# Odd layer of a two-layer decoder trunk: q and k of a head group projected as a pair with seven block products, attention placed between parts of the next values' projection

## Chip, cores and metric

One Trainium2 chip, the kernel on one of its cores. The metric is the device time of one execution in microseconds (us). The kernel before takes 2124.32 us, the median of three runs (2123.64 to 2124.78).

## Reference

The trunk has two layers over a residual stream h of 256 positions and width 2048, all float32. The even layer (sliding-window attention beside a matrix memory) is untouched by the change. The odd layer and the feed-forward block that follows each mixer, cut to what matters:

```python
def forgetting_attention_mixer(xn, w_in, b_f, w_out):
    proj = xn @ w_in                              # 2048 x (2048 + 2048 + 2048 + 16)
    q, k, v, f = split_cols(proj, FOX_SIZES)      # 16 heads of 128
    ...
    log_f = jax.nn.log_sigmoid(f + b_f)
    c = jnp.cumsum(log_f, axis=1)
    ...
        s = q @ k.T * scale + c[query] - c[key]   # causal
        p = jax.nn.softmax(s, axis=-1)
        return p @ v
    ...
    return out @ w_out

h = h + mixer(rms_norm(h, norm_mix[layer]))
h = h + (silu(xn @ w_gate) * (xn @ w_up)) @ w_down   # hidden width 5632
```

## The kernel before

**Numbers as pairs.** Each float32 operand of a large projection is split into a rounded part "hi" and a remainder "lo". The product is three matmuls: hi by hi, hi by lo, lo by hi (lines 179 to 181 in `gemm`, 358 to 360 in `three`). Activations lie transposed in 16 k tiles of 128 (xh and xl for the normed stream, mh and ml for the mixer's or block's result). A weight chunk is two k tiles by 512 columns. It is loaded by the SP queue (`load_raw`, line 107) into one of four buffers "raw", rounded by ScalarE (line 151), and its remainder is made by VectorE (line 152). There are six buffers each for hi and lo. The 256 positions are two blocks of 128 rows (t = 0 and 1), and each accumulates in its own PSUM bank. There are eight banks: four under the tag "acc" (pool pa), four under "pm" (pool pm).

**Pairs with seven products.** In the feed-forward block two matrices are projected together (`pair_group`, line 365). For a pair of k tiles, two row blocks and two matrices make a 2 x 2 by 2 x 2 block product. A plain pair does all eight block products, 24 matmuls. A mixed pair (lines 389 to 419) forms sums of the blocks of x beforehand (`sums_of`, line 214) and differences of the weight blocks on VectorE (lines 396, 397, 401, 402), and does seven, 21 matmuls. Four banks "prod" collect products that must be recombined (lines 420 to 426). The table `ORDER` (line 36) says which of the eight k pairs are mixed: 2, 3 and 6. A pair group so takes all eight banks, four for the plain sums and four for the products.

**The odd layer** (lines 830 to 909). First a narrow projection of 272 columns yields the last two heads' values and the gates f. From the gates come the cumulative sums, which go through DRAM to be broadcast as the bias `cb1` of all 16 heads (2 MB, line 874), and two selections on GpSimd set the causal mask (line 877). Then four head groups of four heads follow. For each: q is projected alone (16 k tiles, 96 matmuls), scaled on ScalarE (line 836) and transposed per head on TensorE (`transpose_many`, line 261); k likewise; v is projected; and `attention` (line 268) does the scores (lines 275, 282), bias and scale on VectorE (276, 283), maximum (289), exponentials on ScalarE (304), normalisation (317), transposes of the probabilities (325, 329), the product with v (333, 334) and the split into mh and ml (343).

**Order of the work.** Each engine runs its instructions in the order of its own queue. The order is not that of the program text: a scheduler places instructions on the engines by its own model, so that those of a group's attention stand among the matmuls of the next projections. `close_layer` (line 550) opens the pool fp0 or fp1 for the rest of a layer (output projection, feed-forward block), in which the block sums `sx` of the normed stream lie too. The odd layer's pool "od" takes the room of the closed fp0.

Of the kernel before, what the change touches and what calls it, by code (L numbers as in the profile page):

```python
# [17 lines left out]
P = 128  # L18
# [21 lines left out]
}  # L40
DOWN_END = ((0, 0), (0, 1), (1, 2), (0, 3), (1, 4), (0, 5), (0, 6), (0, 7))
MID = 6
MID_DOWN = 5
# [11 lines left out]
def trunk(  # L55
# [48 lines left out]

    def load_raw(w, k0, c0, n, pool=wr):
        raw = pool.tile([P, CK, NB], F32, tag="raw", name="raw", bufs=4 if pool is wr else RAWS)
# [107 lines left out]
    def sums_of(pool, sh, sl, copies, full=None):  # L214
        if full is None:
            full = pool.tile([P, 2, NT, P], F32, tag="tmp", name="full")
            copies(full.rearrange("p i t q -> p i (t q)"))
        s = pool.tile([P, 4, P], F32, tag="tmp", name="s4")
        nc.vector.tensor_tensor(out=s[:, 0, :], in0=full[:, 0, 1, :], in1=full[:, 1, 1, :], op=ALU.add)
# [40 lines left out]

    def transpose_many(dst, srcs):
        m = len(srcs)
        pt = pm.tile([P, 4, P], F32, tag="pm", name="ptm")
# [4 lines left out]
    def attention(sp, q_of, k_of, v_of, dv, scale, bias0, bias1, k_tile, sinks=None, negc=None):  # L268
        s = sp.tile([P, 4, 3 * P], F32, tag="s", name="s", bufs=2)
        for half in range(2):  # L270
            hs = slice(half, 4, 2)
            p0 = pm.tile([P, 2, P], F32, tag="pm", name="p0")
            for jj in range(2):
                j = 2 * jj + half
                nc.tensor.matmul(p0[:, jj, :], q_of(j, 0), k_of(j)[:, 0:P], start=True, stop=True)
            nc.vector.scalar_tensor_tensor(
                out=s[:, hs, 0:P], in0=p0, scalar=scale, in1=bias0[:, hs, :], op0=ALU.mult, op1=ALU.add
            )
            p1 = pm.tile([P, 2, S], F32, tag="pm", name="p1")
# [34 lines left out]
        for b in range(NT):  # L314
            for j in range(4):
                e = s[:, j, parts[b]]
                nc.vector.tensor_scalar(e, e, rec[:, b, j : j + 1], None, op0=ALU.mult)
        t0 = sp.tile([P, 4, S], F32, tag="t0", name="t0", bufs=1)
        t1 = sp.tile([P, 4, P], F32, tag="t1", name="t1", bufs=1)
# [12 lines left out]
        def pv(po, j):  # L332
            nc.tensor.matmul(po, v_of(j, 0), t0[:, j, :], start=True, stop=False)  # L333
            nc.tensor.matmul(po[:, P : 2 * P], v_of(j, 1), t1[:, j, :], start=False, stop=True)

        per = P // dv
        for q in range(0, 4 // per, 2):
# [6 lines left out]

    def out_proj(w, idx, key, extra):
        last = KT - 4
        for n0 in (0, 2):
            accs = [new_acc() for _ in range(2)]
            for i in range(2):
                gemm(accs[i], m_of, w, (n0 + i) * NB, NB, 0, last, KT)  # L350
            for i in range(2):
# [12 lines left out]

    def pair_group(fp, par, lhs, sums, mats, order, todo=()):
        plain = [[bank(par, "acc") for _ in range(NT)] for _ in range(2)]
# [4 lines left out]
        for pos, (kind, pair) in enumerate(order):  # L371
# [18 lines left out]
            if first:  # L390
                prods = [bank(1 - par, "prod") for _ in range(4)]
            ra, rb = (load_raw(w, k0, c0, NB, fp) for w, c0 in mats)
            hg, lg = split_chunk(ra, NB)
            run_due(todo, pos)
            t4 = fp.tile([P, 2, NB], F32, tag="t4", name="t4", bufs=1)
            nc.vector.tensor_tensor(out=t4[:, 0, :], in0=rb[:, 0, :], in1=ra[:, 0, :], op=ALU.subtract)
# [7 lines left out]
            for two in (t4, rb):  # L404
                hs = fp.tile([P, 2, NB], F32R, tag="ht", name="ht")
                ls = fp.tile([P, 2, NB], F32R, tag="lt", name="lt")
# [12 lines left out]
            three(plain[0][1], xb[:, t1], lb[:, t1], ht[3], lt[3], False, False)  # L419
        c = fp.tile([P, 4, NB], F32, tag="c", name="c", bufs=1)  # L420
        u2 = fp.tile([P, NB], F32, tag="tmp", name="u2")
        nc.scalar.copy(c[:, 0, :], prods[0])
# [6 lines left out]
    def ffn(layer, fp, sx, sd, key, idx_next=None, key_next=None, finish=None):  # L429
        r = rstd(key)  # L430

        def sums_x(pair):
# [3 lines left out]
        for g0, g1 in zip(PARTS, PARTS[1:]):  # L436
# [4 lines left out]
            for g in range(g0, g1):  # L441
                par = (g1 - 1 - g) % 2
                plain, c = pair_group(
                    fp, par, x_of, sums_x, [(w_gate[layer], g * NB), (w_up[layer], g * NB)], ORDER, todo
                )
# [73 lines left out]
            for n0 in (0, 2):  # L519
                if end and idx_next is None and n0 == 2:  # L520
# [5 lines left out]
                plain, c = pair_group(  # L526
                    fp,
                    1 - n0 // 2,
# [20 lines left out]

    def close_layer(layer, w_out, idx, key, **rest):  # L550
        with tc.tile_pool(name=f"fp{layer}", bufs=2) as fp:
            nx = len(mixed_of(ORDER))
            nd = max(len(mixed_of(o)) for o in DOWN.values())
            sx = [fp.tile([P, nx, 4, P], F32R, name=f"sx{i}", bufs=1) for i in range(2)]
            sd = [fp.tile([P, nd, 4, P], F32R, name=f"sd{i}", bufs=1) for i in range(2)]
            out_proj(w_out, idx, key, (*sx, fp))
            ffn(layer, fp, sx, sd, key, **rest)
# [19 lines left out]
    with tc.tile_pool(name="ev", bufs=1) as ev:  # L577
# [22 lines left out]
        with tc.tile_pool(name="sw", bufs=1) as sw:  # L600
# [17 lines left out]
            def swa(g, qn):  # L618
# [14 lines left out]
                def half_of(j):  # L633
                    return slice((j % 2) * HD, (j % 2 + 1) * HD)

                attention(
                    sw,
# [8 lines left out]
                    sinks=sink[:, 4 * g : 4 * g + 4],  # L646
                )

# [67 lines left out]
        with tc.tile_pool(name="mp", bufs=1) as mp:  # L716
# [99 lines left out]
            for g in range(2):  # L816
# [8 lines left out]
                mlstm(2 * g + 1)  # L825

    close_layer(0, w_out_even[0], 2, "f0", idx_next=1, key_next="m1")


    r1 = rstd("m1")  # L830
    wi1 = w_in_odd[0]
    with tc.tile_pool(name="od", bufs=1) as od:
# [24 lines left out]
        nc.vector.scalar_tensor_tensor(out=nl, in0=fg, scalar=0.0, in1=nl, op0=ALU.min, op1=ALU.subtract)  # L857
        nc.vector.tensor_scalar(nl, nl, -1.0, None, op0=ALU.mult)
        pc = pm.tile([P, NB], F32, tag="pm", name="pcf")
        nc.tensor.matmul(pc[:, 0:FOX_H], upper, nl[:, 0, :], start=True, stop=True)  # L860
# [11 lines left out]
        nc.gpsimd.dma_start(scratch, negct)  # L872
        cb1 = od.tile([P, FOX_H, S], F32, name="cb1")
        nc.gpsimd.dma_start(cb1, scratch.partition_broadcast(P))
        cb0 = od.tile([P, FOX_H, P], F32, name="cb0")
        for dst, src in ((cb0, cb1[:, :, 0:P]), (cb1[:, :, P:S], cb1[:, :, P:S])):
            nc.gpsimd.affine_select(
                out=dst, in_=src, pattern=[[0, FOX_H], [-1, P]], compare_op=ALU.is_ge, fill=NEG, base=0, channel_multiplier=1
            )

        for i in range(4):
            qt = od.tile([P, 4, S], F32, tag="qt", name="qtf")
            kt = od.tile([P, 4, S], F32, tag="kt", name="ktf")
            for off, dst in ((0, qt), (FOX_H * FD, kt)):
                n_ = nat1(project(wi1, off + i * NB, NB), NB, "qk")
                for g in range(0, 4, 2):
                    transpose_many(
                        dst[:, g : g + 2, :].rearrange("p g (t q) -> p (g t) q", q=P),
                        [n_[:, t, (g + u) * FD : (g + u + 1) * FD] for u in range(2) for t in range(NT)],
                    )  # L890
# [6 lines left out]

            attention(
                od,
# [4 lines left out]
                FD**-0.5,  # L904
                cb0[:, 4 * i : 4 * i + 4, :],
                cb1[:, 4 * i : 4 * i + 4, :],
                4 * i,
                negc=negc[:, :, 4 * i : 4 * i + 4],
            )

# [29 lines left out]

    close_layer(1, w_out_odd[0], 3, "f1", finish=finish)

# [48 lines left out]
```

## Time and profile before

| | us |
|---|---|
| median of the runs | 2124.32 |
| profiled execution, its own time | 2125.9 |
| its span, first to last instruction | 2124.2 |
| TensorE (PE) busy | 2105.4 |
| VectorE (DVE) busy | 1709.8 |
| ScalarE (ACT) busy | 1252.2 |

The granted clock of TensorE was 0.998 of full speed on the mean. The odd layer's weights are loaded from 1014.5 us (first issue) on, and its four head groups are worked on from about 1062 to 1346 us.

The page's first part has busy time by engine. The second cuts the span into 40 slices of 53.1 us and gives busy tenths in each. The fourth follows what ended last back to the start. Queries of the trace give groups of instructions by line ("busy, mean ns of one, idle before them"), the waits of an engine and the timeline of a stretch. PE is TensorE's matmul, PEld its weight load, SP the queue that issues loads. A matmul's row is longer than the step from one to the next, since matmuls are pipelined. L152 is line 152 of the kernel.

### The profile page before, as it was taken

The page shows a single profiled execution, that of the slowest core. Times are in us where ns is not written, and L with a number is a line of the kernel's source. Part 1 is how long each engine was busy: PE and PEld are TensorE (multiplying, and loading weights), DVE is VectorE, ACT ScalarE, POOL GpSimd, SP SyncE. Part 2 cuts the span into 40 slices and gives each one's busy share as a digit, 9 for nine tenths or more (in the row PEclk, how much of TensorE's full clock was granted, in tenths as well). Part 3 has the DMA queues.
Part 4 walks back from the last instruction along what each step waited for, and adds up shares of the span by engine and source line. Part 5 has one row for each costly group of instructions (what it writes and reads, how often), then busy time and mean ns, then how long its engine had stood idle before and what let it go on. Part 6 is the DMA issues. An engine that isn't in the chain of part 4 may idle for free.

```text
span 2124.2 us, 26790 instructions
## 1 busy us (share of the span) xinstructions
PE 2105.4 (99%) x9708; PEld 1747.6 (82%) x9708; DVE 1709.8 (80%) x2204; ACT 1252.2 (59%) x1592; POOL 39.6 (2%) x61
## 2 busy tenths in 40 slices
PE   8999999999999999999999999999999999999998
PEld 6888888888888888888888888888888888888886
DVE  6665577899999999999755555668899998999995
ACT  6564455665577656666645444556755667556763
POOL 2010000000000000000010000000000000000000
PEclk9999999999999999999999999999999999999999
DMA  9454555766577666665575564656656767656763
GB/s 310 143 173 142 174 193 190 219 194 205 192 224 222 213 196 216 221 205 189 171 237 163 166 178 148 229 176 193 212 193 218 228 198 205 224 196 208 226 205 134
DMA packets 257989, 420.95 MB, mean 198 GB/s; under 512 B 56464, under 2 KB 64704, under 8 KB 257728
## 3 DMA queue, kind: packets, MB, share of 16 engines
q1 hardware_dynamic: 256976, 415.49, 61.5%
q0 software_dynamic: 736, 3.71, 0.6%
q8 instruction: 76, 1.25, 0.2%
q14 instruction: 57, 0.47, 0.1%
q10 hardware_dynamic: 144, 0.03, 0.0%
HBM read 406.57 MB, written 2.11 MB: 192 GB/s over the span
## 4 chain that ended last, share of the span: by engine, by line
PE 97%; DMA 1%; DVE 1%; ACT 0%; issue 0%; SPq 0%; DVEq 0%; POOLq 0%; POOL 0%; ACTq 0%
PE acc L358 17%; PE acc L359 17%; PE acc L360 17%; PE acc L181 11%; PE acc L180 11%; PE acc L179 11%; PE prod L359 4%; PE prod L358 4%; PE prod L360 4%; PE ptm L265 1%; PE p L282 1%; PE po L333 1%; PE pt L231 0%; DMA raw<-in_w_up_dram 0%; DMA xc<-in_xt_dram 0%; PE pp L325 0%
## 5 line engine op out<-in xcount | busy, mean ns | idle before, releaser
L151 ACT CAST hi<-raw 128x1024 fp32r<-128x1024 f32 (+2 forms) x682 | 695.9, 1032 | 575.3 <-PE acc L181 252.3
L152 DVE TENSOR_TENSOR lo<-raw,hi 128x1024 fp32r<-128x1024 f32 (+2 forms) x682 | 810.6, 1200 | 246.6 <-ACT hi L151 244.5
L359 PE MATMUL acc<-lo,xh 128*128 128x512 f32 x946 | 368.1, 389 | 0.0
L358 PE MATMUL acc<-hi,xh 128*128 128x512 f32 x946 | 365.1, 390 | 0.9 <-DVE u L423 0.9
L360 PE MATMUL acc<-hi,xl 128*128 128x512 f32 x946 | 363.2, 389 | 0.0
L179 PE MATMUL acc<-hi,xh 128*128 128x512 f32 (+3 forms) x736 | 275.7, 377 | 7.1 <-ACT hi L151 7.1
L180 PE MATMUL acc<-lo,xh 128*128 128x512 f32 (+3 forms) x736 | 275.8, 375 | 1.0 <-DVE lo L152 0.9
L181 PE MATMUL acc<-hi,xl 128*128 128x512 f32 (+3 forms) x736 | 276.3, 377 | 0.0
L358 PEld LDWEIGHTS acc<-hi,xh 128*128 128x128 f32 x946 | 177.6, 188 | 38.7 <-DVE u L423 1.8
L359 PEld LDWEIGHTS acc<-lo,xh 128*128 128x128 f32 x946 | 177.6, 188 | 36.8 <-DVE lo L152 0.2
L360 PEld LDWEIGHTS acc<-hi,xl 128*128 128x128 f32 x946 | 177.5, 188 | 36.9
L359 PE MATMUL acc<-lo,mh 128*128 128x512 f32 x444 | 173.1, 390 | 0.0
L360 PE MATMUL acc<-hi,ml 128*128 128x512 f32 x444 | 171.1, 389 | 0.0
L358 PE MATMUL acc<-hi,mh 128*128 128x512 f32 x444 | 170.1, 389 | 0.0
L179 PEld LDWEIGHTS acc<-hi,xh 128*128 128x128 f32 x736 | 138.9, 189 | 30.2 <-ACT hi L151 7.3
L180 PEld LDWEIGHTS acc<-lo,xh 128*128 128x128 f32 x736 | 139.1, 189 | 26.5 <-DVE lo L152 2.9
L181 PEld LDWEIGHTS acc<-hi,xl 128*128 128x128 f32 x736 | 138.8, 189 | 25.6 <-issue 1.9
L253 ACT CAST ht<-raw 128x1024 fp32r<-128x1024 f32 x94 | 98.7, 1050 | 52.3 <-issue 20.9
L254 DVE TENSOR_TENSOR lt<-raw,ht 128x1024 fp32r<-128x1024 f32 x94 | 114.6, 1219 | 16.6 <-ACT ht L253 16.2
L179 PE MATMUL acc<-hi,mh 128*128 128x512 f32 x320 | 125.7, 393 | 1.2 <-ACT mh L253 1.2
L180 PE MATMUL acc<-lo,mh 128*128 128x512 f32 x320 | 125.7, 393 | 0.0
L181 PE MATMUL acc<-hi,ml 128*128 128x512 f32 x320 | 124.0, 390 | 0.0
(307 smaller groups left out, 3075.3 us busy)
## 6 DMA issues: line engine op xcount, KB each, us to landing
raw<-in_w_gate_dram SPq DMA_DIRECT2D x176, 512.0 KB, 4.4
raw<-in_w_up_dram SPq DMA_DIRECT2D x176, 512.0 KB, 4.6
raw<-in_w_down_dram SPq DMA_DIRECT2D x176, 512.0 KB, 4.8
raw<-in_w_in_odd_dram SPq DMA_DIRECT2D x88, 512.0 KB, 3.8
raw<-in_w_in_even_dram SPq DMA_DIRECT2D x64, 512.0 KB, 4.8
raw<-in_w_out_even_dram SPq DMA_DIRECT2D x32, 512.0 KB, 3.6
raw<-in_w_out_odd_dram SPq DMA_DIRECT2D x32, 512.0 KB, 3.9
raw<-in_w_in_odd_dram SPq DMA_DIRECT2D x8, 272.0 KB, 2.9
```

Of the source, the lines that this page charges most:

```text
L151: latest[0] = nc.scalar.copy(hi[:, :, 0:n], raw[:, :, 0:n])
L152: nc.vector.tensor_tensor(out=lo[:, :, 0:n], in0=raw[:, :, 0:n], in1=hi[:, :, 0:n].bitcast(F32), op=ALU.subtract)
L179: nc.tensor.matmul(o, ah[:, ts], hi, start=(k == 0), stop=False)
L180: nc.tensor.matmul(o, ah[:, ts], lo, start=False, stop=False)
L181: nc.tensor.matmul(o, al[:, ts], hi, start=False, stop=(k == k_all - 1))
L253: nc.scalar.copy(dst_h, src)
L254: nc.vector.tensor_tensor(out=dst_l, in0=src, in1=dst_h.bitcast(F32), op=ALU.subtract)
L265: nc.tensor.transpose(pt[:, i, :], s_, ident)
L282: nc.tensor.matmul(p1[:, jj, :], q_of(j, 1), k_of(j), start=True, stop=True)
L358: nc.tensor.matmul(o, ah, hi, start=start, stop=False)
L359: nc.tensor.matmul(o, ah, lo, start=False, stop=False)
L360: nc.tensor.matmul(o, al, hi, start=False, stop=stop)
```

## The change

It has five parts.

1. **q and k as a pair.** For each head group the 512 columns of q and the 512 of k go through `pair_group` as the two matrices, with the table `QK_ORDER`: k pairs 2, 3 and 6 mixed, five plain. The sums of both parts are scaled and added into c (ScalarE scales c, VectorE adds the plain sum). c serves as the natural q and k, and later as the scores of the softmax.
2. **Room.** A class `Room` says where `pair_group` takes its buffers. In the odd layer a mixed pair's first chunk goes to the four common raw buffers and its second to two of its own. The rounded differences lie in the halves of mh and ml that attention has not yet written (k tiles 8 to 15). For the last group only one such half is left, and common hi and lo buffers take the other's place.
3. **Block sums of x.** `sums_from` forms them for three pairs from xh + xl at the start of the odd layer. Their tiles `sx` move out of fp0 and fp1 into a pool that stays open.
4. **Attention in steps.** `attention` becomes a generator with two stops, and the values' projection of the next group (`v_part`, in two pm banks) is written in parts between: four k tiles ahead of the transposes of q and k, four ahead of the scores, eight ahead of the transposes of the probabilities. In the last group the first 12 k tiles of two column blocks of the output projection stand there. Values of group 0 are projected at the start.
5. **Bias by group.** `cb1` holds four heads and is loaded (512 KB) and masked anew for each group.

```diff
+QK_ORDER = ((0, 0), (0, 1), (1, 2), (0, 4), (1, 3), (0, 5), (1, 6), (0, 7))
...
+    class Room:
+        def __init__(self, pool, raws=RAWS, two=None):
+            self.pool, self.raws, self.two_ = pool, raws, two
+
+        def raw(self, m, w, k0, c0):
+            if self.two_ and m == 0:
+                return load_raw(w, k0, c0, NB)
+            return load_raw(w, k0, c0, NB, self.pool, self.raws)
...
+        def two(self):
+            if self.two_:
+                self.two_.append(self.two_.pop(0))
+                if self.two_[-1] is None:
+                    return [wp.tile([P, CK, NB], F32R, tag=tag, name=tag) for tag in ("hi", "lo")]
+                return self.two_[-1]
+            return [self.pool.tile([P, 2, NB], F32R, tag=tag, name=tag, bufs=2) for tag in ("ht", "lt")]
...
+    def sums_from(room, sh, sl, lhs, pair):
+        full = room.tmp([P, 2, NT, P], "full")
+        for i in range(2):
+            a, b = lhs(2 * pair + i)
+            nc.vector.tensor_tensor(
+                out=full[:, i, :, :].rearrange("p t q -> p (t q)"), in0=a.bitcast(F32), in1=b.bitcast(F32), op=ALU.add
+            )
+        sums_of(room.pool, sh, sl, None, full)
...
+        halves = [
+            [m[:, k : k + 4, :].rearrange("p (a b) s -> p a (b s)", a=2) for m in (mh, ml)] for k in (8, 12)
+        ]
+        room = Room(od, 2, halves)
...
+        first = v_part(0)
+        first(0, 8)
...
+        first(8, KT)
         for i in range(4):
...
-            for off, dst in ((0, qt), (FOX_H * FD, kt)):
-                n_ = nat1(project(wi1, off + i * NB, NB), NB, "qk")
+            cb1 = od.tile([P, 4, S], F32, tag="cb1", name="cb1", bufs=1)
+            nc.gpsimd.dma_start(cb1, scratch[4 * i : 4 * i + 4, :].partition_broadcast(P))
...
+            if i == 3:
+                halves[:] = [halves[1], None]
+            plain, c = pair_group(
+                room, 0, x_of, sums_q, [(wi1, i * NB), (wi1, FOX_H * FD + i * NB)], QK_ORDER
+            )
+            for m in range(2):
+                for t in range(NT):
+                    o = c[:, 2 * m + t, :]
+                    nc.scalar.mul(o, o, r1[:, t : t + 1])
+                    nc.vector.scalar_tensor_tensor(
+                        out=o, in0=plain[m][t], scalar=r1[:, t : t + 1], in1=o, op0=ALU.mult, op1=ALU.add
+                    )
+            if i < 3:
+                part = v_part(i + 1)
+                fillers = [lambda k=k: part(k, k + 4) for k in (0, 4)] + [lambda: part(8, KT), lambda: None]
+            else:
+                begun = [new_acc() for _ in range(2)]
...
+                fillers = [begin(0, 0, 4), begin(0, 4, 8), both(begin(0, 8, 12), begin(1, 0, 4)), begin(1, 4, 12)]
+            ps = (pa, "acc") if i < 3 else (pm, "pm")
+            fillers.pop(0)()
...
-            vn = nat1(project(wi1, c_v + i * NB, NB if i < 3 else VT), NB if i < 3 else VT, "vn")
+            vn = vns[i]
...
-            attention(
+            fillers.pop(0)()
+            for _ in attention(
...
+                s=c[:, :, 0 : 3 * P],
+                ps=ps,
+            ):
+                fillers.pop(0)()
```

More of the change, by code (lines that the diff above doesn't have):

```diff
@@ L430, in ffn @@
         r = rstd(key)
+        room = Room(fp)
         def sums_x(pair):
@@ L825, in trunk @@
                 mlstm(2 * g + 1)
+    late = ctx.enter_context(tc.tile_pool(name="late", bufs=1))
+    sx = [late.tile([P, len(mixed_of(ORDER)), 4, P], F32R, name=f"sx{i}") for i in range(2)]
     close_layer(0, w_out_even[0], 2, "f0", idx_next=1, key_next="m1")
@@ L858, in trunk, with sums_q, v_part, part @@
         nc.vector.tensor_scalar(nl, nl, -1.0, None, op0=ALU.mult)
+        halves = [
+            [m[:, k : k + 4, :].rearrange("p (a b) s -> p a (b s)", a=2) for m in (mh, ml)] for k in (8, 12)
+        ]
+        room = Room(od, 2, halves)
+        mixed = mixed_of(QK_ORDER)
+        for j, pair in enumerate(mixed):
+            sums_from(room, sx[0][:, j, :, :], sx[1][:, j, :, :], x_of, pair)
+        def sums_q(pair):
+            j = mixed.index(pair)
+            return sx[0][:, j, :, :], sx[1][:, j, :, :]
+        vns = {}
+        def v_part(i):
+            vw = NB if i < 3 else VT
+            acc = [bank(1, "vacc") for _ in range(NT)]
+            def part(k0, k1):
+                gemm(acc, x_of, wi1, c_v + i * NB, vw, k0, k1, KT)
+                if k1 == KT:
+                    vns[i] = nat1(acc, vw, "vn", bufs=2)
+            return part
+        first = v_part(0)
+        first(0, 8)
         pc = pm.tile([P, NB], F32, tag="pm", name="pcf")
```

96 lines of the change are left out of this document (55 added, 41 removed).

## The prediction

> **What bounds the kernel now.** I read the page first: shares, slices, chain.
>
> ```profile
> span 2124.2 us, 26790 instructions
> ...
> PE 2105.4 (99%) x9708; PEld 1747.6 (82%) x9708; DVE 1709.8 (80%) x2204; ACT 1252.2 (59%) x1592; POOL 39.6 (2%) x61
> ...
> DVE  6665577899999999999755555668899998999995
> ...
> PE 97%; DMA 1%; DVE 1%; ACT 0%; issue 0%; SPq 0%; DVEq 0%; POOLq 0%; POOL 0%; ACTq 0%
> ```
>
> TensorE is busy for 2105.4 of 2124.2 us and is 97% of the chain that ended last. VectorE sits in the nineties in the feed-forward stages and in the fifties in slices 20 to 24 (1062 to 1327 us), which are the odd layer's mixer. Busy time of matmuls is modelled, so I next read stretches and the waits of TensorE: one stretch of the feed-forward part, the entry into the odd layer, and three of the four head groups (columns: stretch, then us busy and instructions of PE, PEld, DVE, ACT, POOL, then clock and DMA).
>
> ```profile
> 560.00:760.00 200.00, 199.53 (x881) 164.81 (x880) 187.50 (x233) 129.11 (x140) 0.00 (x0) 1.00 0.67 212
> ...
> 1012.00:1062.00 50.00, 50.00 (x278) 43.48 (x277) 35.99 (x55) 31.16 (x49) 0.69 (x1) 1.00 0.59 173
> 1062.00:1133.00 71.00, 71.00 (x326) 58.98 (x326) 39.35 (x48) 34.82 (x48) 6.13 (x4) 1.00 0.65 208
> ...
> 1204.00:1275.00 71.00, 71.00 (x337) 59.31 (x336) 38.24 (x41) 31.83 (x46) 0.00 (x0) 1.00 0.58 171
> 1275.00:1346.00 71.00, 71.00 (x387) 61.46 (x386) 40.87 (x60) 34.84 (x59) 0.00 (x0) 1.00 0.50 159
> ```
>
> ```profile
> PE acc L179 <- ACT hi L151: 7.1, 1, 7.1
> ...
> PE acc L358 <- DVE u L423: 0.9, 2, 0.5
> ```
>
> A head group takes 71.0 us and TensorE is busy for all of it. So attention's chains are already covered by other matmuls: the steps of the change cannot win an idle time, since there is none there. All of TensorE's named waits make some 10 us in the whole run, the longest (7.1 us) at the start of the program. What the change can win is matmuls; what it can lose is the cover.
>
> What does one matmul cost? The timeline of TensorE inside a feed-forward group: first and last of 25 starts in a row, product blocks and plain ones mixed.
>
> ```profile
> 600.41 0.39 PE L360 MATMUL prod<-ht,sx 128*128 128x512 f32 x1
> ...
> 605.85 0.39 PE L358 MATMUL acc<-hi,xh 128*128 128x512 f32 x1
> ```
>
> 24 steps in 5.44 us are 0.2267 us each; the 0.39 us of a row overlaps its neighbours. The Trainium skill, page "TensorE: Matmul & The Clock Gate", section "Wait — 56ns, not 53.3ns?", has 215.7 ns for this width when warm. This trace, at full clock, differs by 11 ns; by the page's figure the sum below would be 7.8 instead of 8.2 us.
>
> **Matmuls removed.** A plain pair of k tiles costs 2 matrices x 4 blocks x 3 matmuls = 24; the seven products cost 21. Three mixed pairs in each of four groups remove 3 x 3 x 4 = 36 matmuls, and the built kernel's TensorE list is indeed 36 shorter (9537 to 9501). 36 x 0.2267 = **8.16 us**, 2.04 per group: 71.0 becomes 69.0. Everything else on TensorE (values, transposes, scores, output projection) is moved, not removed. Nothing after the odd mixer changes but its start.
>
> **VectorE and ScalarE added.** VectorE's groups in the same feed-forward stretch (the last numbers: busy, mean ns):
>
> ```profile
> L152 DVE TENSOR_TENSOR lo<-raw,hi 128x1024 fp32r<-128x1024 f32 x62 | 74.4, 1217 | 2.1 <-ACT hi L151 2.1
> L254 DVE TENSOR_TENSOR lt<-raw,ht 128x1024 fp32r<-128x1024 f32 x15 | 18.3, 1219 | 2.3 <-ACT ht L253 2.2
> ...
> L401 DVE TENSOR_TENSOR raw<-raw,t 128x512 f32<-128x512 f32 x15 | 10.2, 683 | 0.0
> ...
> L254 DVE TENSOR_TENSOR lo<-raw,hi 128x512 fp32r<-128x512 f32 x14 | 9.6, 684 | 3.0 <-ACT hi L253 3.0
> ...
> L454 DVE SCALAR_TENSOR_TENSOR c<-c,r 128x512 f32<-128x512 f32 x8 | 5.9, 742 | 0.0
> ...
> L424 DVE TENSOR_TENSOR c<-prod,u 128x512 f32<-128x512 f32 x5 | 3.4, 683 | 0.0
> ```
>
> A mixed pair costs VectorE three whole-chunk remainders (3 x 1.22), one half (0.68) and four differences (4 x 0.68): 7.1 us, against 2.4 for a plain pair. Three pairs add 14.0 us; recombining adds 4 x 0.68 = 2.7, scaling the sums (as L454) 4 x 0.74 = 3.0. A group has 38.2 + 19.7 = 58 us of VectorE work in 69 us: 84%. The feed-forward stretch runs 187.5 in 200 (94%) with the same pairs, and TensorE there waits for nearly nothing. So VectorE's amount of work costs **nothing**. ScalarE gains some 6 us on 32: nothing either.
>
> **Softmax chain.** After the change the last transposes of the scores stand behind 45 value matmuls and 33 of the next pair group: 78 x 0.2267 = 17.7 us after the last score matmul (groups 0 and 1). What must end in that time is read from VectorE and ScalarE in group 1 of before:
>
> ```profile
> 1192.65 0.42 DVE L276 SCALAR_TENSOR_TENSOR s<-p,cb 128x256 f32<-128x256 f32 x1 [0.86 <-PE p L275]
> ...
> 1196.19 1.80 DVE L289 TENSOR_REDUCE mx<-s 128x4 f32<-128x512 f32 x2
> ...
> 1202.44 1.93 DVE L317 TENSOR_SCALAR s<-s,rec 128x128 f32<-128x128 f32 x8
> ```
>
> The chain took 11.7 us there (1192.65 to 1204.37), with two chunk remainders (2 x 1.22) between. In the changed order some eight foreign operations stand in VectorE's queue before the reciprocal: four differences and four remainders, 4 x 0.68 + 4 x 1.22 = 7.6 us; two of the remainders replace those already there, and some run beside the exponentials. So 11.7 + 7.6 - 2.4 = 16.9 at most, against 17.7 plus the score matmuls themselves: about 1 to 2 us are left. In the last such step (group 2 under group 3) the value matmuls are half as wide, and the rest by the same count is about 1 us. I take 0 here; the other end is 1 us for each of three groups, 3 us.
>
> **Entry into the layer.** Here VectorE gets work while it has no room: it runs nearly without a gap from the first row to the second, the last remainders of x.
>
> ```profile
> 1030.21 0.69 DVE L423 TENSOR_TENSOR u<-prod,c 128x512 f32<-128x512 f32 x1 [3.39 <-PE prod L360]
> ...
> 1047.02 0.47 DVE L237 SCALAR_TENSOR_TENSOR xl<-pt,gT,xh 128x256 fp32r<-128x256 f32 x1
> ```
>
> ```profile
> L219 DVE TENSOR_TENSOR s<-c x14: 281/284/293, 454.7 to 2056.0; 128x128 f32<-128x128 f32 x14
> ...
> L254 DVE TENSOR_TENSOR sd<-s,sd x16: 679/682/686, 462.4 to 2064.2; 128x512 fp32r<-128x512 f32 x16
> ```
>
> The block sums of x cost 3 x (2 additions of 128x256, which the trace lacks and I take at the 0.47 of the row above, + 4 x 0.28 + 0.68) = 8.2 us in all. In the built order four additions, four block differences and one difference of weights stand before the last remainder of x: 1.9 + 1.1 + 0.7 = 3.7 us later for the last x. TensorE has value matmuls to fill with, whose chunks are also late. Bounds 0 and 3.7 us; I take **0.8**, nearer to 0, because in before this stretch had as narrow a queue and TensorE was busy in all 50.0 us of it.
>
> **Loads.** A mixed pair's second chunk goes to two new buffers, the first to the four old ones, where it is held longer.
>
> ```profile
> raw<-in_w_in_odd_dram SPq DMA_DIRECT2D x88, 512.0 KB, 3.8
> ...
> DMA to landing us min/median/max: 2.7/3.7/10.7
> ```
>
> A mixed and a plain pair take TensorE (21 + 24) x 0.2267 = 10.2 us; two buffers turn round in 20.4, enough for the slowest landing (10.7) and the 7.1 of VectorE. SP is passed in order: the first two such loads stand ahead of the last narrow chunk and wait for the closed feed-forward pool. Cost 0; without this cover a landing of 3.8 would show.
>
> **GpSimd.** The mask's 2 MB load and two selections become four of each at a quarter of the size, each due a group (60 us) later. The trace shows what a selection does to VectorE:
>
> ```profile
> 1079.81 4.96 POOL L877 TENSOR_SCALAR_AFFINE_SELECT cb<-cb 128x2048 f32<-128x2048 f32 x2 [10.46 <-DMA cb<-scratch]
> ```
>
> ```profile
> 1060.42 2.36 DVE L152 TENSOR_TENSOR lo<-raw,hi 128x1024 fp32r<-128x1024 f32 x2 [0.53 <-ACT hi L151]
> ...
> 1083.13 3.95 DVE L152 TENSOR_TENSOR lo<-raw,hi 128x1024 fp32r<-128x1024 f32 x2 [0.22 <-ACT hi L151]
> ```
>
> Two remainders that take 2.36 us took 3.95 beside it: 1.6 us lost, till the selection ended. In the change this falls into the softmax chain, 5.0 / 4 = 1.25 us per group at most. The Trainium skill, page "SBUF — State Buffer", section "Who interferes with whom", says that a VectorE instruction with two inputs in SBUF and a GpSimd instruction that reads SBUF exclude each other for a whole instruction; the 3.95 us agrees. I take 0, with 5.0 us in all as the other end.
>
> **Sum.** -8.16 + 0.8 = -7.4 us against the profiled span of 2124.2. The profiled execution took 2125.9, the runs' median is 2124.32, 0.1% apart; taken from the median: **2117.0 us**.
>
> **Rivals.**
> 1. The cover is too thin: the entry costs 3.7 and the softmax steps 3 us. For it: only 1 to 2 us are left in each step. Against it: before had narrow steps and no wait. 2124.3 - 8.2 + 6.7 = 2122.8.
> 2. VectorE is held by GpSimd in the middle of each softmax chain and this reaches TensorE whole: 2124.3 - 7.4 + 5.0 = 2121.9. Against it: VectorE has 11 us spare per group, and only what exceeds the 1 to 2 us left counts.
> 3. Slower: loads. The SP queue stops at a load whose buffer a mixed pair still holds, and plain chunks behind it come late. 12 mixed pairs; the change breaks even when each costs 8.16 / 12 = 0.7 us, and is slower by over 0.2% from 1.03 us each. One median landing uncovered in every second pair, 6 x 3.8 = 23 us, gives 2139. For it: fewer buffers than the feed-forward part has, and a slowest landing of 10.7. Against: the 20.4 us turn.
> 4. More is won: transposes in runs of 16 instead of between matmuls, or waits smaller than taken. Without the 0.8 and with 1 us from the transposes: 2115.1 or a little less. This lies at the low end of the forecast; below 2114.5 I know no mechanism.
>
> **How the numbers follow.** A measurement of this kernel tells some 0.2% (4.25 us) from no change, so "faster" is below 2120.1. Forecast (2114.5 to 2120.1) 0.64; rival 4 beyond that 0.04; rival 1 0.15; rival 2 0.04; rival 3 0.13. Faster 0.68, same 0.19, slower 0.13. The range 2114.5 to 2122.0 holds the forecast and most of rivals 1 and 2, some 0.8.
>
> **What would show it.** Right: 36 fewer matmuls, groups of 69 us with TensorE busy throughout, VectorE near 58 us in each. Wrong: waits of TensorE for the score transposes' input (softmax), for chunk remainders near 1045 us (entry), or of ScalarE's casts for loads of the odd weights (rival 3). A pitch in the odd layer other than 0.227 us would make the sum itself wrong.

## The result, and the profile after

| | before | after |
|---|---|---|
| median of the runs side by side (7 each), us | 2124.66 | 2117.72 |
| lowest to highest, us | 2123.64 to 2125.28 | 2115.86 to 2119.16 |
| profiled execution, us | 2125.9 | 2117.76 |
| its span, us | 2124.2 | 2116.1 |

After stands to before as 0.9967, 95% interval 0.9956 to 0.9979. The medians differ by 6.94 us. The forecast was 2117.0, so it is off by 0.7 us. The two spans differ by more (8.1 us), because the profiled execution of before was 1.2 us above the median in the table.

The page of after, in the same parts as before:

```profile
span 2116.1 us, 26910 instructions
...
PE 2098.3 (99%) x9672; PEld 1742.4 (82%) x9672; DVE 1783.9 (84%) x2329; ACT 1272.5 (60%) x1623; POOL 49.2 (2%) x70
...
DVE  6666567899999998999877878778999998998995
...
PE 98%; DMA 1%; DVE 0%; issue 0%; ACT 0%; POOLq 0%; POOL 0%; SPq 0%; ACTq 0%
```

TensorE has 36 matmuls fewer and is busy 7.1 us less. VectorE has 74 us more work, and its slices in the odd mixer rise from fives to sevens and eights. TensorE is still the chain.

The stretches of after (columns as in the prediction: stretch, its length, then us busy and instructions of PE, PEld, DVE, ACT, POOL, then clock, DMA share and GB/s):

```profile
1010.00:1060.00 50.00, 49.20 (x267) 42.60 (x266) 41.63 (x72) 29.88 (x51) 0.69 (x1) 1.00 0.65 192
1060.00:1128.00 68.00, 68.00 (x315) 56.51 (x314) 53.15 (x63) 38.30 (x44) 3.89 (x4) 1.00 0.69 209
1128.00:1196.00 68.00, 68.00 (x324) 57.02 (x324) 55.85 (x73) 39.20 (x57) 3.44 (x3) 1.00 0.62 186
1196.00:1264.00 68.00, 68.00 (x341) 57.81 (x340) 52.85 (x74) 36.27 (x57) 3.70 (x3) 1.00 0.53 158
1264.00:1332.00 68.00, 68.00 (x349) 58.02 (x349) 53.58 (x70) 38.44 (x57) 4.69 (x3) 1.00 0.55 175
```

In the four head groups TensorE is busy in all of 272 us, at full clock. Only the entry (first row) shows a gap, 0.8 us. All of TensorE's waits in the whole run (us in total, times, longest) say which it is:

```profile
PE acc L181 <- ACT hi L153: 7.1, 1, 7.1
PE acc L181 <- ACT mh L255: 1.2, 1, 1.2
PE acc L181 <- ACT xh L238: 0.5, 1, 0.5
PE acc L183 <- DVE xl L239: 0.3, 1, 0.3
```

The first two are the start of the program and a wait outside the odd mixer. The last two are the late x of the odd layer, 0.5 + 0.3 us.

Where did the time come from? Two marks that both kernels have enclose the odd mixer: the last Silu of layer 0's feed-forward block and the first of layer 1's, in ScalarE's timeline. Before:

```profile
957.58 0.73 ACT L452 ACTIVATE c<-c,r 128x512 f32<-128x512 f32 x1
...
1468.16 0.73 ACT L452 ACTIVATE c<-c,r 128x512 f32<-128x512 f32 x1
```

After:

```profile
956.82 0.73 ACT L495 ACTIVATE c<-c,r 128x512 f32<-128x512 f32 x1
...
1460.26 0.73 ACT L495 ACTIVATE c<-c,r 128x512 f32<-128x512 f32 x1
```

510.6 us became 503.4: 7.1 us were won between the marks. Of the rest of the spans' difference 0.8 us lie ahead of the first mark and 0.2 behind the second, where the change does nothing.

### The profile page after: what moved, and what is told of

Its sections match the earlier page's. It is cut to its first block, busy times and chain, and to the rows that moved or that the text cites. A ratio compares the mean times of both kernels' runs of the same rounds, so it can differ in the third digit from the quotient of the medians.

```text
span 2116.1 us, 26910 instructions
## 1 busy us (share of the span) xinstructions
PE 2098.3 (99%) x9672; PEld 1742.4 (82%) x9672; DVE 1783.9 (84%) x2329; ACT 1272.5 (60%) x1623; POOL 49.2 (2%) x70
## 3 DMA queue, kind: packets, MB, share of 16 engines
q0 software_dynamic: 1168, 3.71, 0.6%
q8 instruction: 76, 1.25, 0.2%
## 4 chain that ended last, share of the span: by engine, by line
PE 98%; DMA 1%; DVE 0%; issue 0%; ACT 0%; POOLq 0%; POOL 0%; SPq 0%; ACTq 0%
PE acc L366 19%; PE acc L367 19%; PE acc L368 19%; PE acc L183 7%; PE acc L181 7%; PE acc L182 7%; PE prod L367 5%; PE prod L368 5%; PE prod L366 5%; PE vacc L181 1%; PE vacc L183 1%; PE vacc L182 1%; PE ptm L267 1%; PE p L285 1%; PE po L337 1%; PE pt L233 0%
## 5 line engine op out<-in xcount | busy, mean ns | idle before, releaser
L367 PE MATMUL acc<-lo,xh 128*128 128x512 f32 x1121 | 436.6, 389 | 0.0
L366 PEld LDWEIGHTS acc<-hi,xh 128*128 128x128 f32 x1121 | 210.3, 188 | 44.3 <-DVE u L465 0.8
L368 PEld LDWEIGHTS acc<-hi,xl 128*128 128x128 f32 x1121 | 210.4, 188 | 43.7
L367 PEld LDWEIGHTS acc<-lo,xh 128*128 128x128 f32 x1121 | 210.4, 188 | 43.6
L181 PE MATMUL acc<-hi,xh 128*128 128x512 f32 (+3 forms) x352 | 128.9, 370 | 7.7 <-ACT hi L153 7.1
L183 PE MATMUL acc<-hi,xl 128*128 128x512 f32 (+3 forms) x352 | 129.6, 370 | 0.3 <-DVE xl L239 0.3
L182 PE MATMUL acc<-lo,xh 128*128 128x512 f32 (+3 forms) x352 | 129.8, 369 | 0.0
L255 ACT CAST ht<-t 128x1024 fp32r<-128x1024 f32 x94 | 98.8, 1051 | 38.4 <-PE prod L368 27.3
L256 DVE TENSOR_TENSOR lt<-t,ht 128x1024 fp32r<-128x1024 f32 x94 | 114.3, 1216 | 7.8 <-ACT ht L255 7.8
L255 ACT CAST hi<-raw 128x512 fp32r<-128x512 f32 (+1 forms) x109 | 68.8, 631 | 74.5 <-PE acc L368 63.5
```

Of the source, the lines that this page charges most:

```text
L181: nc.tensor.matmul(o, ah[:, ts], hi, start=(k == 0), stop=False)
L182: nc.tensor.matmul(o, ah[:, ts], lo, start=False, stop=False)
L183: nc.tensor.matmul(o, al[:, ts], hi, start=False, stop=(k == k_all - 1))
L255: nc.scalar.copy(dst_h, src)
L256: nc.vector.tensor_tensor(out=dst_l, in0=src, in1=dst_h.bitcast(F32), op=ALU.subtract)
L366: nc.tensor.matmul(o, ah, hi, start=start, stop=False)
```

## The experiments

The kernel before ran beside each group of runs, with medians of 2125.12 (e1 to e4), 2125.25 (e5 to e8) and 2124.81 us (e9 to e12). Ratios are to it, with 95% intervals.

| run | median us | ratio | interval |
|---|---|---|---|
| e1_all_plain | 2125.54 | 1.0002 | 0.9993 to 1.0011 |
| e2_four_mixed | 2130.38 | 1.0026 | 1.0016 to 1.0036 |
| e3_selects_twice | 2118.56 | 0.9970 | 0.9959 to 0.9982 |
| e4_no_steps | 2148.02 | 1.0108 | 1.0094 to 1.0122 |
| e5_four_mixed_late | 2134.97 | 1.0045 | 1.0032 to 1.0058 |
| e6_no_third_part | 2121.71 | 0.9982 | 0.9973 to 0.9991 |
| e7_sums_late | 2118.30 | 0.9968 | 0.9956 to 0.9981 |
| e8_three_raws | 2117.57 | 0.9965 | 0.9952 to 0.9977 |
| e9_three_adjacent | 2122.11 | 0.9984 | 0.9975 to 0.9993 |
| e10_none_ahead_of_transposes | 2118.88 | 0.9970 | 0.9959 to 0.9982 |
| e11_adjacent_third_set | 2117.73 | 0.9966 | 0.9954 to 0.9978 |
| e12_after_again (unchanged) | 2116.28 | 0.9961 | 0.9949 to 0.9974 |

### All pairs plain

```diff
-QK_ORDER = ((0, 0), (0, 1), (1, 2), (0, 4), (1, 3), (0, 5), (1, 6), (0, 7))
+QK_ORDER = ((0, 0), (0, 1), (0, 2), (0, 4), (0, 3), (0, 5), (0, 6), (0, 7))
...
+        if prods is None:
+            return plain, c
...
-                    nc.scalar.mul(o, o, r1[:, t : t + 1])
-                    nc.vector.scalar_tensor_tensor(
...
+                    nc.scalar.mul(o, plain[m][t], r1[:, t : t + 1])
```

> All eight k pairs of q and k plain, everything else as in the changed kernel (pair group, steps, bias by group); the 36 matmuls are back, the recombination is gone, the block sums of x are still formed but unused. Theory (the time is the number of matmuls times 0.2267 us plus TensorE's named waits): 2117.7 + 8.2 = 2125.9, TensorE's waits in the odd layer still under 1 us. Rival (the steps of the attention made the gain): it stays below 2121.

Measured 2125.54, as expected. Everything of the change but the seven products is in this kernel: pairing, steps, bias by group. It has the 9708 matmuls of before and its time. So the whole gain belongs to the mixed pairs. Its stretch of the second group:

```profile
1128.00:1196.00 68.00, 68.00 (x316) 56.82 (x315) 35.53 (x43) 34.27 (x50) 1.77 (x3) 1.00 0.59 177
```

VectorE works 35.5 us here and 55.9 us in the changed kernel, and TensorE is busy for all 68.00 us in both: 20 us more VectorE work in this stretch cost nothing.

### Four mixed pairs, in two orders

If VectorE has room, a fourth mixed pair should win 12 matmuls more. The sums of the fourth pair lie in two further tiles `more`. In e2 the mixed pairs stand near one another, in e5 the first stands later and three stand in a row:

```diff
-QK_ORDER = ((0, 0), (0, 1), (1, 2), (0, 4), (1, 3), (0, 5), (1, 6), (0, 7))
+QK_ORDER = ((0, 0), (1, 2), (0, 1), (1, 3), (1, 5), (0, 4), (1, 6), (0, 7))   # e2
+QK_ORDER = ((0, 0), (0, 1), (1, 2), (0, 4), (1, 3), (1, 5), (1, 6), (0, 7))   # e5
...
+        more = [od.tile([P, len(mixed) - 3, 4, P], F32R, name=f"more{i}") for i in range(2)]
```

> Four k pairs of q and k mixed instead of three, 12 matmuls fewer. Theory: 2117.7 - 2.7 = 2115.0, VectorE about 59 us of a group's 65 (90%), which the feed-forward part bears too. Rival (the cover is used up: only 1.3 to 1.6 us are left before the score transposes): TensorE waits 1 to 2 us in each group for the normalised scores or for differences of weights, and the time is 2117 to 2121.

> Again four mixed pairs of q and k, but the first two pairs of a group stay plain as in the changed kernel (plain, plain, mixed, plain, mixed, mixed, mixed, plain). Place theory (the run with four mixed pairs lost because its mixed pair in second place took 24 plain matmuls, 5.4 us, from the cover of the previous group's softmax): 2115 to 2117. Load theory (a fourth mixed pair is more than VectorE and ScalarE can prepare in time, wherever it stands): 2121 or more, TensorE waiting for differences of weights.

Measured 2130.38 and 2134.97: both missed, both slower than before. Both have 9660 matmuls, 12 fewer than the changed kernel. TensorE's longest waits in e5 outside the program's start:

```profile
PE prod L366 <- ACT mh L255: 4.5, 6, 1.3
PE acc L366 <- ACT hi L255: 2.5, 2, 1.4
```

What is behind them shows one of these places in slices of 4 us (e5, group 1):

```profile
1164.00:1168.00 4.00, 4.00 (x20) 3.33 (x19) 1.29 (x3) 0.59 (x1) 0.00 (x0) 1.00 0.00 0
1168.00:1172.00 4.00, 3.79 (x17) 2.68 (x17) 1.09 (x1) 2.58 (x3) 0.00 (x0) 1.00 0.00 0
1172.00:1176.00 4.00, 2.85 (x11) 1.89 (x12) 3.93 (x7) 1.04 (x1) 0.00 (x0) 1.00 0.38 108
1176.00:1180.00 4.00, 2.94 (x8) 2.07 (x7) 3.61 (x5) 3.20 (x4) 0.00 (x0) 0.67 0.49 154
```

Read it from top to bottom, slice by slice. From 1164 to 1172 nothing is loaded (last two columns) and VectorE works 2.4 of 8 us. Only then TensorE runs dry, some 2.4 us in all from 1168 on, and then its clock is down to 0.67 for a slice. So VectorE isn't short of time; it stands still. Its timeline, ScalarE's and the SP queue's at that place:

```profile
1164.77 0.69 DVE L256 TENSOR_TENSOR ml<-po,mh 128x512 fp32r<-128x512 f32 x1 [0.17 <-ACT mh L255]
1170.91 1.23 DVE L256 TENSOR_TENSOR ml<-t,mh 128x1024 fp32r<-128x1024 f32 x1 [5.45 <-ACT mh L255]
1172.05 1.22 DVE L256 TENSOR_TENSOR ml<-raw,mh 128x1024 fp32r<-128x1024 f32 x1
```

```profile
1169.15 0.59 ACT L464 COPY c<-prod 128x512 f32<-128x512 f32 x1 [4.41 <-PE prod L368]
1169.83 1.05 ACT L255 CAST mh<-t 128x1024 fp32r<-128x1024 f32 x1
```

```profile
1173.30 8.71 SPq L109 DMA_DIRECT2D raw<-in_w_in_odd_dram  x4
```

The SP queue's own wait there (us, times, longest):

```profile
SPq L109 <- DVE ml L256: 13.9, 1, 13.9
```

VectorE is held for 5.45 us at the remainder of a difference ("ml<-t,mh"). It waits for ScalarE's rounding, which stands in ScalarE's queue behind a copy that waits 4.41 us for a product of TensorE. (The copy need not be the only reason: a product that reads mh ends at 1169.79, 0.04 us ahead of the rounding, so the buffer may have held it as well; the trace doesn't separate the two.) Behind it in VectorE's queue stands the remainder that reads a raw buffer of the mixed pair ("ml<-raw,mh", ends at 1173.27). The SP queue, passed in order, had stopped at the load into that buffer, and goes on at 1173.30, with the plain chunks behind. So: a product, ScalarE's copy and rounding, a remainder and only then a load, and by the time that it lands TensorE has run dry. In e2 the loads stop in the same way from 1236 to 1244 us (VectorE held for 4.78 us at "ml<-t,mh") and from 1304 to 1312 us (held for 4.87 us at the remainder of attention's result). In addition e2 has the wait that its rival expected, for the normalised scores ("PE pp L329 <- DVE c L320"), but only once, 1.9 us, of 9.2 us that TensorE is idle from 1060 to 1400 us. In e5, where the first two pairs of a group are plain again, this wait is gone, and the run is slower still.

### Selections twice

```diff
-            for dst, src in ((cb0, cb1[:, :, 0:P]), (cb1[:, :, P:S], cb1[:, :, P:S])):
+            for dst, src in ((cb0, cb1[:, :, 0:P]), (cb1[:, :, P:S], cb1[:, :, P:S]), (cb0, cb0), (cb1[:, :, P:S], cb1[:, :, P:S])):
```

> Each GpSimd selection of the mask is done twice (the second changes nothing). GpSimd takes 12.9 us for the eight selections in the changed kernel, some 25 here. Theory: VectorE's time is not the end of any chain, and the 1.3 us left per group takes most of the hold: 2117.7 to 2119. Rival (what GpSimd holds of VectorE reaches TensorE): the 13 us more of GpSimd cost 4 to 13 us, 2122 to 2131.

Measured 2118.56, and TensorE's waits in the groups show nothing new. GpSimd is busy 57.5 us instead of 49.2, 8 us more and not 13. Rival 2 falls.

### Attention in one piece

```diff
-            fillers.pop(0)()
+            while fillers:
+                fillers.pop(0)()
...
-            fillers.pop(0)()
             for _ in attention(
...
-                fillers.pop(0)()
+                pass
```

> The parts of the next values' projection (last group: of the output projection) all stand ahead of the transposes of q and k; attention is written in one piece. Same matmuls. Theory: the scores' chain of 17 us loses the 45 value matmuls (10.2 us) as cover and has only the next group's first two plain pairs, 48 x 0.2267 = 10.9 us, before the banks run out: waits of about 6 us in each of three groups or more, 2130 to 2142. Rival (the scheduler finds other cover by itself, as it did in the kernel before): 2117 to 2120.

Measured 2148.02, some 6 us beyond the expected range. TensorE's waits:

```profile
PE p L278 <- DVE ktf L268: 12.6, 5, 5.2
PE pp L329 <- DVE c L320: 7.2, 1, 7.2
...
PE acc L366 <- DVE c L279: 1.6, 1, 1.6
```

21.4 us of waits appear where there were none: the scores wait for the transposed k, and in one group the probabilities' transposes wait for the normalisation. The span is 28.5 us longer. By the page, TensorE is idle 21.6 us more (2144.6 - 2105.2 against 2116.1 - 2098.3) and busy 6.9 us more with the same 9672 matmuls. The expectation had no term for these 6.9 us; the mean granted clock, 0.995 against 0.998, makes some 6 of them (an estimate). So the cover of the steps is real.

### One step taken away

In e6 the third part moves ahead of the scores, so that none is written between softmax and the transposes of the probabilities. In e10 no part is written ahead of the transposes of q and k, and two stand ahead of the scores.

```diff
+            fillers.pop(0)()   # e6: one more ahead of the scores
             for _ in attention(
...
-                fillers.pop(0)()
+                if len(fillers) > 0:
+                    fillers.pop(0)()
```

```diff
-            fillers.pop(0)()   # e10: the one ahead of the transposes of q and k
...
+            fillers.pop(0)()   # and one more ahead of the scores
             for _ in attention(
```

> The part of the next values' projection that stands ahead of the transposes of the scores (eight k tiles) is put ahead of the scores instead; the parts ahead of the transposes of q and k stay. In the last group the output projection's last part moves up into that place. Theory: the softmax chain of some 17 us keeps only the next group's first plain pairs, 33 to 48 matmuls or 7.5 to 10.9 us, as cover: 6 to 9 us of wait for the normalised scores in each of groups 0 to 2, none for the copies of k: 2136 to 2145. Rival (the scheduler refills): 2117 to 2121.

> No part of the next values' projection ahead of the transposes of q and k; both of the first two parts stand ahead of the scores. Theory: after its last matmul a group's sums still need a scaling and an addition for each of four tiles (some 3 us) before the transposes, which nothing covers now: TensorE waits 2 to 3 us in each of four groups, 2126 to 2130. Rival (the scheduler refills, as it did without the third part): 2117 to 2120.

Measured 2121.71 and 2118.88. My theory (each part covers its own wait) missed both. The rival (the scheduler refills the gap with other matmuls) holds for e10; e6 lies 0.7 us beyond its range, but the refilling is there: in group 1 of e6, 64 matmuls of the next pair group stand between the scores and the transposes of the probabilities (1139.5 to 1154.1 us), where the changed kernel has 45 of the values and 33 of the pair group. No wait for the normalisation appears. TensorE's longest wait in the odd mixer of e6 is this one:

```profile
PE po L337 <- ACT t L330: 0.4, 1, 0.4
```

By the ratios e6 is some 3 us slower than the changed kernel. What makes them isn't placed; the profiled execution (2119.70 us) was 2.0 us below e6's median and may not show it.

### Entry and loads

```diff
-        for j, pair in enumerate(mixed):   # e7: moved behind first(8, KT)
-            sums_from(room, sx[0][:, j, :, :], sx[1][:, j, :, :], x_of, pair)
```

```diff
-        room = Room(od, 2, halves)   # e8: a third raw buffer of its own
+        room = Room(od, 3, halves)
```

> The block sums of x are written after the first values' projection instead of before it. Theory: TensorE's waits of 0.5 and 0.3 us at the entry go, 2116.9 or 0.8 less than the changed kernel. Rival: the sums come late for the first mixed pair of group 0, TensorE waits for them there, and the time is the same or more.

> Three buffers of its own instead of two for the second chunk of a mixed pair. Theory: VectorE's four waits for such loads (7.7 us) shrink, and since VectorE ends no chain the time stays 2117.7 within 1. Rival (loads hold the odd layer up): 2 us or more are won.

Measured 2118.30 and 2117.57: nothing won. In e7 the two waits at the entry were expected to go; they are 0.3 + 0.3 us instead of 0.5 + 0.3, hardly less than in a second profile of the changed kernel (e12: 0.4 + 0.3). So where the sums stand in the program doesn't decide it, and no wait for the sums (the rival) appears. In e8 the time was as expected, but VectorE's waits for these loads should have shrunk and didn't. Who waits for the loads of the odd weights, in e8 (us, times):

```profile
  DVE t L439: 11.0, 5
```

In the changed kernel it is 7.7 us in 4 waits. A load that lands late for VectorE isn't late for TensorE here.

### Three mixed pairs next to one another, and a third set of buffers

After e2 and e5 two causes were open: too much work for VectorE, or neighbours that take one another's buffers. e9 keeps three mixed pairs and the amount of work and puts them side by side. e11 adds a third set of difference buffers to it (the common hi and lo, in groups 0 to 2). e12 is the changed kernel beside them.

```diff
-QK_ORDER = ((0, 0), (0, 1), (1, 2), (0, 4), (1, 3), (0, 5), (1, 6), (0, 7))
+QK_ORDER = ((0, 0), (0, 1), (0, 4), (1, 2), (1, 3), (1, 6), (0, 5), (0, 7))   # e9, e11
...
         room = Room(od, 2, halves)
+        halves.append(None)   # e11
```

> Three mixed pairs as in the changed kernel, but next to each other (plain, plain, plain, mixed, mixed, mixed, plain, plain). Same matmuls and same VectorE work. Neighbour theory (both runs with four mixed pairs lost because mixed pairs stood next to each other: each needs the buffers of rounded differences of the one before, and no plain pair covers their refilling): waits of TensorE for differences as there, 2123 to 2131. Load theory (a fourth pair is more work than fits): 2117 to 2119, as the changed kernel.

> As the run with three neighbouring mixed pairs, but in groups 0 to 2 the rounded differences go through three sets of buffers instead of two (the third from the common hi and lo buffers). Neighbour theory by buffers: a large part of that run's loss is won back. If the loss is the preparation itself (VectorE and ScalarE need 7 us for a mixed pair that TensorE does in 4.8), it stays.

> The changed kernel once more beside these runs on their chip, as the base they are compared with: 2117.7, within 1.

Measured 2122.11, 2117.73 and 2116.28. Neighbours alone cost 5.8 us at the same amount of work (4.4 against the first measurement of the changed kernel), and e11 is 4.4 us faster than e9. e12 came out 1.4 us below the same kernel's first median and so outside its own expectation: differences of that size between runs say little. e9 fell between the two expectations, nearest the lower edge of the neighbours' range. Most of its loss is one place, in the last head group; slices of 4 us:

```profile
1296.00:1300.00 4.00, 4.00 (x20) 3.34 (x19) 1.38 (x2) 1.09 (x3) 0.00 (x0) 1.00 0.02 4
1300.00:1304.00 4.00, 3.73 (x17) 2.63 (x15) 1.02 (x1) 1.50 (x2) 0.00 (x0) 1.00 0.00 0
1304.00:1308.00 4.00, 1.93 (x6) 0.97 (x6) 3.90 (x6) 2.03 (x3) 0.00 (x0) 1.00 0.00 0
1308.00:1312.00 4.00, 3.88 (x10) 3.06 (x11) 3.59 (x4) 3.85 (x5) 0.00 (x0) 0.57 0.51 147
```

It is e5's picture again: no loads for 12 us, VectorE held, then TensorE idle for 2.1 us, then a clock of 0.57. VectorE is held at the same instruction, and ScalarE's rounding before it waits for a product too:

```profile
1302.98 1.23 DVE L256 TENSOR_TENSOR ml<-t,mh 128x1024 fp32r<-128x1024 f32 x1 [5.02 <-ACT mh L255]
```

```profile
1301.90 1.05 ACT L255 CAST mh<-t 128x1024 fp32r<-128x1024 f32 x1 [1.45 <-PE prod L368]
```

The rounding takes nothing from that product, so what it waits for is the buffer mh, which the product reads.

It is tempting to say that e11 shows the cure, since VectorE waits 1.98 us at this instruction there, and TensorE is busy for 67.79 of the 68 us from 1264 on (e9: 65.55). But this place lies in the last group, and there e11 has the same two sets of buffers as e9: the line `halves[:] = [halves[1], None]` sets them anew, and the third set serves groups 0 to 2 alone, in which e9's trace shows no loss (TensorE busy in all 204 us from 1060 to 1264). The rounding waits for the same buffer in e11 too, until nearly the same time:

```profile
1301.46 1.05 ACT L255 CAST mh<-t 128x1024 fp32r<-128x1024 f32 x1 [2.24 <-PE prod L368]
```

What differs is what TensorE still has to do. In e11 the group's products start at 1275.67 us instead of 1272.49, and those that need no differences of weights last until 1306 us; in e9 the last of them ends at 1301 us, and soon TensorE has nothing left. So the expectation "a large part is won back" came true, but not shown is that the third set did it: the last group came 3 us later against the same wait, and why stays open. Shown is that this order costs time at the same work (it also moves the first mixed pair one place back), and that where TensorE runs dry VectorE had been held by a rounding that waits for a buffer. For four pairs, e2 and e5 show the same stop of the loads behind a held VectorE; how much of their 13 and 17 us the buffers make stays open as well. None of these versions beats the changed kernel by more than the runs can tell.

## Why the prediction was right

**Matmuls removed (8.16 us).** Right. The odd layer's matmuls keep the pitch; first and last of 32 starts in a row in group 2 of the changed kernel, product blocks and plain ones mixed:

```profile
1244.77 0.39 PE L367 MATMUL acc<-lo,xh 128*128 128x512 f32 x1
...
1251.80 0.39 PE L368 MATMUL prod<-mh,sx 128*128 128x512 f32 x1
```

7.03 us in 31 steps are 0.2268 us. The all-plain run gives the gain back whole. The sign "groups of 69 us" can't be read off a single group: from one group's first score to the next it is 71.7, 66.7 and 73.1 us (before 73.9, 73.9 and 63.5), since what stands between them differs (values of the next group, and in the last group of the changed kernel parts of the output projection). -8.16 + 0.8 = -7.4 stands against -7.1 between the two marks and -6.9 of the medians; the remaining 0.3 to 0.5 us are less than the runs can tell. The other figure that the prediction weighed (215.7 ns, the Trainium skill, page "TensorE: Matmul & The Clock Gate", section "Wait — 56ns, not 53.3ns?") would give -7.0 and can't be told apart by the time, but the pitch in the odd layer is the trace's 0.227.

**VectorE's work (0).** Right, and shown by the all-plain run against the changed one. The 58 us per group of 69 were 1 to 4 us too many (52.9 to 55.9 in 68).

**Softmax chain (0, with 1 to 2 us left).** Right in size too. Group 1 of the changed kernel, VectorE and then TensorE:

```profile
1201.55 0.42 DVE L279 SCALAR_TENSOR_TENSOR c<-p,cb 128x256 f32<-128x256 f32 x1
...
1208.61 0.62 DVE L300 TENSOR_TENSOR mx<-mx,negc 128x8 f32<-128x8 f32 x1
...
1215.03 0.69 DVE L439 TENSOR_TENSOR t<-raw 128x512 f32<-128x512 f32 x1 [2.40 <-DMA raw<-in_w_in_odd_dram]
...
1216.59 1.93 DVE L320 TENSOR_SCALAR c<-c,rec 128x128 f32<-128x128 f32 x8
```

```profile
1220.12 0.27 PE L329 MATMUL pp<-ident,c 128*128 128x128 f32 x1
```

The chain takes 17.0 us (1201.55 to 1218.52; "16.9 at most") and ends 1.6 us ahead of the first transpose. That the sum was met to 0.1 us is partly luck, since it lacked a term: VectorE waits 2.40 us for a load ahead of the reciprocal, which starts at 1216.37, 1.2 us after the last exponential (1215.15). A thin rest is not fatal by itself: taking one part away made the scheduler bring others (e6, e10). The wait came when no part was left (e4, 7.2 us in one group), and once in e2 (1.9 us).

**Entry (0.8, bounds 0 and 3.7).** Right: 0.5 + 0.3 us. That it is 0.8 to the tenth is luck, since the figure was chosen between the bounds and not worked out. The two VectorE rows that the prediction used, in the changed kernel:

```profile
1029.45 0.69 DVE L465 TENSOR_TENSOR u<-prod,c 128x512 f32<-128x512 f32 x1 [3.39 <-PE prod L368]
...
1049.17 0.47 DVE L239 SCALAR_TENSOR_TENSOR xl<-pt,gT,xh 128x256 fp32r<-128x256 f32 x1
```

19.7 us lie between them, against 16.8: the last x is 2.9 us later (3.7 predicted), and TensorE fills all but 0.8 us.

**Loads (0).** Right for this order of the pairs, as far as TensorE goes. VectorE does wait for them (7.7 us in four places, one of them in the chain above), under cover. A third raw buffer won nothing.

**GpSimd (0; at most 5.0).** The cost was right, the term behind it mis-sized. "1.25 us per group at most" took a quarter of the old selections. The changed kernel's selections in GpSimd's timeline, all four groups (two in each row):

```profile
1080.74 2.72 POOL L952 TENSOR_SCALAR_AFFINE_SELECT cb<-cb 128x512 f32<-128x512 f32 x2 [3.44 <-DMA cb<-scratch]
...
1136.99 2.89 POOL L952 TENSOR_SCALAR_AFFINE_SELECT cb<-cb 128x512 f32<-128x512 f32 x2 [3.52 <-DMA cb<-scratch]
...
1208.34 3.15 POOL L952 TENSOR_SCALAR_AFFINE_SELECT cb<-cb 128x512 f32<-128x512 f32 x2 [3.15 <-DMA cb<-scratch]
...
1275.02 4.13 POOL L952 TENSOR_SCALAR_AFFINE_SELECT cb<-cb 128x512 f32<-128x512 f32 x2 [3.90 <-DMA cb<-scratch]
```

They take 12.9 us, not 5.0. Had TensorE no cover there, the bound would have been too low.

**Rivals.** 1 falls: the waits it priced at 6.7 us are 0.8. 2 falls by e3. 4 isn't seen: what was expected of the transposes didn't show as a gain. 3, loads stopped by a buffer that a mixed pair holds, costs TensorE nothing in the changed kernel. But it is what the traces show where a step further is slower (e2, e5, e9). The prediction named the held buffer and priced the stop by a load's landing (3.8 us); what holds the buffer longer is VectorE's queue, stopped at a remainder whose rounding waits for an earlier product.

## What to carry to other kernels

Where one engine is busy throughout, count its instructions and price them by their pitch; work added on other engines is free while it has cover, and the all-plain kind of run (all of the change but the removed instructions) shows both at once. A busy share below 100% doesn't say that another such step is free: look for the in-order queue that would be held, and at what is released only behind it. When TensorE runs dry for a little, go back in slices of a few us to the slice in which the loads stopped, and look at which engine is held there and what releases it. And before a run is taken as proof of a cause, see whether its edit reaches the place where the time was lost: e11's does not.

## What the runs showed of the hardware

**A short gap costs more than itself.** In e9 TensorE lost 2.07 us in one slice of 4 us, and the next slice ran at a granted clock of 0.57. TensorE's rows in it:

```profile
1309.01 0.63 PE L367 MATMUL prod<-ml,sx 128*128 128x512 f32 x1
1309.44 0.63 PE L368 MATMUL prod<-mh,sx 128*128 128x512 f32 x1
```

The step is 0.43 instead of 0.227 us. A clock of 0.57 for 4 us loses 0.43 x 4 = 1.7 us on top of the gap. The Trainium skill, page "TensorE: Matmul & The Clock Gate", section "What's actually happening", says that the clock is either full or half, set for windows of about 3.4 us by how busy TensorE was, and half after an idle window; an estimate from this page, 3.4 us at half in a slice of 4, gives 0.57 as well. The trace agrees in size, but here no window of that length was idle throughout.

**Selections beside a busy VectorE.** Two selections of a quarter of the old size take 2.72 to 4.13 us in the changed kernel. In the all-plain run the two of group 1 take 1.22, and VectorE stands still meanwhile (from 1138.1 to 1141.8 us):

```profile
1139.12 1.22 POOL L954 TENSOR_SCALAR_AFFINE_SELECT cb<-cb 128x512 f32<-128x512 f32 x2 [3.48 <-DMA cb<-scratch]
```

It is not VectorE's work as a whole that decides: in e11, with as much of it as in the changed kernel, the selections of groups 1 and 2 fall into such pauses and take 1.22 us too. VectorE's operation on 8 columns at 1208.61 took 0.62 us beside a selection (above); in the kernel before the same operation, with no selection beside it, took 0.17:

```profile
1198.03 0.17 DVE L297 TENSOR_TENSOR mx<-mx,negc 128x8 f32<-128x8 f32 x1
```

So both sides lose where they meet; which loses more isn't settled here.
